# Scheduling a hybrid decoder layer with a second simulated machine: one flag on the tile context

## The chip, the cores and the metric

The kernel runs on one core of one Trainium2 chip. Its time is the device time of the program in microseconds (us), the median of three executions. One more execution was recorded by the hardware profiler. The engines are called PE (TensorE, matrix products), DVE (VectorE), ACT (ScalarE), POOL (GpSimd) and SP (SyncE, which here only issues transfers). PEld is the loading of a matrix product's stationary operand, which overlaps the PE.

## The reference

One decoder layer over 1024 positions of width 1024, all in 32-bit floats. Cut to what matters:

```python
z = rmsnorm(h, norm_mix_g) @ w_in                  # 1024 -> 3840 columns
o_a = hgrn2_mix(a_q, a_f, a_i, a_g, ...)           # 4 heads, gated linear recurrence
o_b = dilated_window_mix(b_q, b_k, b_v)            # 4 heads, three dilated causal windows
o_c = rwkv7_mix(c_in, ...)                         # 4 heads, RWKV-7 recurrence
h = h + concat(o_a, o_b, o_c) @ w_out
h = h + conv_glu_ffn(rmsnorm(h, norm_ffn_g), ffn_up, ffn_conv_w, ffn_conv_b, ffn_down)   # inner width 2816
h = h + sigmoid(rmsnorm(h, norm_ple_g) @ ple_gate) * (p @ ple_proj)
return rmsnorm(h, final_norm_g)
```

## The kernel before, in words

Every activation is held with features on the 128 partitions and positions along the row, in tiles of 128 x 512 (half of the positions) or 128 x 1024. A product of full precision is made of three products of a shorter float format: `split2` (L104 on ACT, L106 on POOL or DVE) cuts a weight tile into a high part `whi` and a low part `wlo`, and `mm3` (L127, L129, L131) adds high x high, high x low and low x high in one accumulator. Six buffers each hold `whi` and `wlo`, two hold a raw weight block `wraw` (512 KB, loaded on the SP queue at L95), and accumulators lie in the eight banks of the matmul memory (two of 128 x 1024 called `dp`, four of 128 x 512 called `mx`).

The stages follow each other:

1. `mix_norm` (L352 to L362) loads the input, makes its operands and the first projections while the norm is still being computed.
2. `rwkv` runs twice, once for each pair of heads: `rwkv_prep` (L478 to L542), `rwkv_inverse` (31 steps of two DVE instructions, L591 and L593, with trips through memory before and after), then `rwkv_main` in four groups of four chunks (L689 to L781). Projections of later blocks are written into the program between these (`project_rest`, 6, 4, 4 and 4 blocks) so that the PE has products to make while the DVE works through the inverse.
3. The HGRN2 heads run as two streams A (heads 0 and 2) and B (heads 1 and 3), the windowed attention as a stream C and the last projections as a stream F. `interleave` steps through these four generators in a fixed list, so their instructions alternate in the program. Inside a head, seven levels follow each other: ACT makes keys (L847), the PE makes scores (L857), the DVE puts them in place under a mask (L859) and scales queries (L862), DVE or POOL scales keys (L860). Then come the state chain (L901, L910), the output (L920, L922), its norm (L927 to L934) and its transposition (L940, L941). Stream C makes scores (L1001), a masked minimum (L1008), an exponential (L1010), transpositions (L1024, L1025) and values (L1037).
4. `phase_out` multiplies by `w_out` and starts the second norm.
5. `phase_up` computes the feed-forward's up-projection in 22 units of seven block products (L1148, Strassen-like), each unit with sums of weight blocks on the DVE (L1254 to L1262), additions out of the accumulators (L1292, L1301, L1303, L1311, L1313), the convolution (L1322 on ACT, L1323 and L1324 on DVE) and the gated product (L1331). The result goes to memory.
6. `phase_down` makes seven products of 11 steps (L1439) with the split of the reloaded operand (L1435, L1436).
7. `phase_ple` makes the gate (L1513 to L1516), the last norm, and writes the output (L1499, L1500).

No order of instructions is written out by hand for an engine. The program is traced in the order of the Python code, and the tile framework orders it when the `with tile.TileContext(nc)` block closes. It plays the program on a simulated machine with a clock. On each engine and on each transfer queue it takes, among the instructions whose operands the simulation says are there and whose buffers are free, the one that stands first in the program. The order in which the simulated machine takes them becomes the fixed order of that engine, and buffers are handed out in that order. Semaphore waits are added afterwards for every dependence, so the order on one engine is what is fixed and the time of each instruction is not. An engine's queue, and a transfer queue, runs strictly in that order: an instruction that waits holds back what stands behind it.

There are two simulated machines to choose from. The kernel before uses the framework's ordinary one. The other one, the timeline simulator, describes each instruction as a list of events on parts of an engine (its sequencer, a queue of issued instructions, the engine itself), on the transfer engines and on the memory interface that DVE and POOL share. It is chosen by one argument of the context.

## Time and profile before

| | |
|---|---|
| time, median of 3 runs | 1546.66 us |
| the three runs | 1538.52, 1546.66, 1549.97 us |
| span of the profiled execution, first to last instruction | 1541.8 us |
| instructions in it | 20120 |
| PE busy | 1478.3 us (96%), 7480 products |
| PEld busy | 1223.3 us (79%) |
| DVE busy | 1096.9 us (71%), 1578 instructions |
| ACT busy | 630.1 us (41%), 1079 instructions |
| POOL busy | 425.3 us (28%), 353 instructions |
| transfers | 167.83 MB, mean 109 GB/s |

The time of the profiled execution itself is not recorded beside its span; the span lies 4.9 us under the median of the three runs and between the lowest and the highest of them. In a row of the profile, "idle before" is the time that an engine stood still ahead of the instructions of that row, and the arrow names what ended the wait. A product's end is modelled, and products are pipelined, so the mean time of one (some 390 ns) is longer than the distance from one start to the next.

### The profile page before, as it was taken

The page shows a single profiled execution, that of the slowest core. Times are in us where ns is not written, and L with a number is a line of the kernel's source. Part 1 is how long each engine was busy: PE and PEld are TensorE (multiplying, and loading weights), DVE is VectorE, ACT ScalarE, POOL GpSimd, SP SyncE. Part 2 cuts the span into 40 slices and gives each one's busy share as a digit, 9 for nine tenths or more (in the row PEclk, how much of TensorE's full clock was granted, in tenths as well). Part 3 has the DMA queues.
Part 4 walks back from the last instruction along what each step waited for, and adds up shares of the span by engine and source line. Part 5 has one row for each costly group of instructions (what it writes and reads, how often), then busy time and mean ns, then how long its engine had stood idle before and what let it go on. Part 6 is the DMA issues. An engine that isn't in the chain of part 4 may idle for free.

```text
span 1541.8 us, 20120 instructions
## 1 busy us (share of the span) xinstructions
PE 1478.3 (96%) x7480; PEld 1223.3 (79%) x7480; DVE 1096.9 (71%) x1578; ACT 630.1 (41%) x1079; POOL 425.3 (28%) x353
## 2 busy tenths in 40 slices
PE   7999999999999989999999999999999999999996
PEld 5778988877977777777777888888888888888774
DVE  6567452656446567854788888888888799777684
ACT  6521331312323555523554444444444444455541
POOL 2233221323211113212214544444444000003230
PEclk9999999999999999999999999999999999999997
DMA  5124103124034132045342333333332883351352
GB/s 196 58 76 123 41 1 110 41 75 110 1 110 137 35 110 76 28 167 199 119 145 79 106 102 103 103 106 107 105 105 80 298 314 97 109 158 61 103 177 82
DMA packets 78706, 167.83 MB, mean 109 GB/s; under 512 B 19920, under 2 KB 20048, under 8 KB 78608
## 3 DMA queue, kind: packets, MB, share of 16 engines
q1 hardware_dynamic: 65120, 145.97, 29.0%
q10 hardware_dynamic: 12400, 16.52, 3.1%
q0 software_dynamic: 1088, 4.06, 0.8%
q8 instruction: 59, 0.97, 0.3%
q14 instruction: 39, 0.32, 0.1%
HBM read 120.12 MB, written 46.40 MB: 108 GB/s over the span
## 4 chain that ended last, share of the span: by engine, by line
PE 80%; DVE 8%; issue 5%; ACT 3%; DMA 2%; POOL 2%; POOLq 0%; SPq 0%; DVEq 0%; ACTq 0%
PE bg L1148 15%; PE bv L1148 11%; PE dp L131 7%; PE bv L1439 7%; PE bg L1439 7%; PE dp L129 7%; PE dp L127 7%; PE hsc L857 2%; PE swq L1001 1%; PE pgm L751 1%; PE swo L1037 1%; PE swt L1024 1%; PE zp L127 1%; PE zp L129 1%; PE zp L131 1%
## 5 line engine op out<-in xcount | busy, mean ns | idle before, releaser
L127 PE MATMUL dp<-xh,whi 128*128 128x512 f32 x544 | 185.1, 399 | 10.6 <-ACT xh L352 8.9
L131 PE MATMUL dp<-xh,wlo 128*128 128x512 f32 x544 | 184.7, 397 | 1.8 <-DVE wlo L106 1.5
L129 PE MATMUL dp<-xl,whi 128*128 128x512 f32 x544 | 185.9, 399 | 0.3 <-DVE xl L353 0.2
L106 POOL TENSOR_TENSOR wlo<-raw,whi 128x512 fp32r<-128x512 f32 x84 | 135.4, 1631 | 75.7 <-ACT whi L104 75.7
L104 ACT CAST whi<-wraw 128x512 fp32r<-128x512 f32 x120 | 73.3, 619 | 200.9 <-PE dp L129 136.1
L106 POOL TENSOR_TENSOR wlo<-wraw,whi 128x512 fp32r<-128x512 f32 x60 | 82.2, 1369 | 255.7 <-ACT whi L104 250.8
L1148 PE MATMUL bg<-t,whi 128*128 128x512 f32 x352 | 133.2, 389 | 0.0
L127 PEld LDWEIGHTS dp<-xh,whi 128*128 128x128 f32 x544 | 102.4, 190 | 33.1 <-ACT xh L352 8.9
L131 PEld LDWEIGHTS dp<-xh,wlo 128*128 128x128 f32 x544 | 103.4, 191 | 24.1 <-DVE wlo L106 2.0
L129 PEld LDWEIGHTS dp<-xl,whi 128*128 128x128 f32 x544 | 102.8, 190 | 24.3 <-DVE xl L353 2.5
L106 POOL TENSOR_TENSOR wlo<-s,whi 128x512 fp32r<-128x512 f32 x44 | 64.7, 1470 | 172.7 <-ACT whi L104 158.3
L1439 PE MATMUL bg<-t,whi 128*128 128x512 f32 x308 | 95.1, 390 | 0.0
L1439 PE MATMUL bv<-t,whi 128*128 128x512 f32 x308 | 94.9, 389 | 0.0
L104 ACT CAST whi<-raw 128x512 fp32r<-128x512 f32 x88 | 52.6, 619 | 96.8 <-issue 51.2
L104 ACT CAST whi<-s 128x512 fp32r<-128x512 f32 x66 | 38.9, 620 | 121.0 <-PE bg L1148 113.5
L167 POOL TENSOR_TENSOR rst<-rst,mhalf 128x4 f32<-128x4 f32 x8 | 9.3, 1158 | 251.6 <-DVE rst L161 251.5
L1148 PEld LDWEIGHTS bg<-t,whi 128*128 128x128 f32 x352 | 66.1, 188 | 13.8
L106 DVE TENSOR_TENSOR wlo<-wraw,whi 128x512 fp32r<-128x512 f32 x60 | 46.1, 773 | 41.8 <-ACT whi L104 34.7
L1439 PEld LDWEIGHTS bv<-t,whi 128*128 128x128 f32 x308 | 57.8, 188 | 12.0
L1148 PE MATMUL bg<-t,wlo 128*128 128x512 f32 x176 | 67.2, 389 | 0.0
L1439 PEld LDWEIGHTS bg<-t,whi 128*128 128x128 f32 x308 | 57.8, 188 | 11.8
L1435 ACT CAST t<-t 128x512 fp32r<-128x512 f32 x77 | 47.6, 621 | 44.5 <-PE bv L1439 31.1
(404 smaller groups left out, 3720.7 us busy)
## 6 DMA issues: line engine op xcount, KB each, us to landing
raw<-in_ffn_up_dram SPq DMA_DIRECT2D x44, 512.0 KB, 3.7
wraw<-in_w_in_dram SPq DMA_DIRECT2D x30, 512.0 KB, 3.7
z<-zst SPq DMA_DIRECT2D x18, 512.0 KB, 3.1
gb<-ct SPq DMA_DIRECT2D x33, 256.0 KB, 2.3
t<-gb SPq DMA_DIRECT2D x33, 256.0 KB, 2.8
t<-gt SPq DMA_DIRECT2D x33, 256.0 KB, 2.7
zl<-z SPq DMA_DIRECT2D x16, 512.0 KB, 4.2
wraw<-in_ple_gate_dram SPq DMA_DIRECT2D x16, 512.0 KB, 3.6
```

Source lines behind the costliest of these rows:

```text
L104: nc.scalar.copy(hi, src)
L106: eng.tensor_tensor(lo, src, hi.bitcast(F32), ALU.subtract)
L127: nc.tensor.matmul(ps[hf], wh, xh[hf], start=first, stop=False)
L129: nc.tensor.matmul(ps[hf], wh, xl[hf], start=False, stop=False)
L131: nc.tensor.matmul(ps[hf], wl, xh[hf], start=False, stop=last)
L751: nc.tensor.matmul(pg[:, u, :], X[:, 2 * hh + u, 0:128], RB[:, 2 * hh + u, :], start=True, stop=True)
L857: nc.tensor.matmul(sc[:, c, :], ks[:, c * P:(c + 1) * P], view(qt, c * P, [2 * n, 64 // n], [HT + n, 2], [1, n]), start=True, stop=True)
L1001: nc.tensor.matmul(pq[h][:, b:b + w], d["q"][hs, qb * P:nk], d["k"][hs, b:b + w], start=True, stop=True)
L1024: nc.tensor.transpose(pt[:, kb * P:(kb + 1) * P], lg[:, b + kb * P:b + (kb + 1) * P], self.ident)
L1148: nc.tensor.matmul(ps, w[part == 2][:, s], X[k][part == 1], start=start and k == part == 0, stop=k == 3 and part == 2, skip_group_check=no ...
L1435: nc.scalar.copy(xh, x)
L1439: nc.tensor.matmul(ps[m], wt[part == 2][:, m * P:(m + 1) * P], (xh, xl)[part == 1], start=k == part == 0, stop=k == NK - 1 and part == 2)
```

## The change

The context is built with one more argument. The traced program, its operations, tiles, pools and transfers stay as they are; the order of instructions on every engine and queue, and which of a pool's buffers a tile gets, come from the timeline simulator.

```diff
--- before.py
+++ after.py
@@ -1585,7 +1585,7 @@
         arrays[f"in_{name}_dram"] = v
         args[name] = nc.dram_tensor(f"in_{name}_dram", v.shape, mybir.dt.from_np(v.dtype), kind="ExternalInput").ap()
     out = nc.dram_tensor("out_0_dram", (ND, P, T), F32, kind="ExternalOutput").ap()
-    with tile.TileContext(nc) as tc:
+    with tile.TileContext(nc, schedule_with_timeline_sim=True) as tc:
         Trunk(tc, args, out).build()
     r = _run(nc, [arrays], core_ids=[0])
     y = r.results[0]["out_0_dram"]
```

## The prediction

> **What bounds the kernel now.** I read the page's busy times first, then the same by stage, then the chain that ended last, then the waits inside the one stage where the PE is not full.
>
> ```profile
> span 1541.8 us, 20120 instructions
> PE 1478.3 (96%) x7480; PEld 1223.3 (79%) x7480; DVE 1096.9 (71%) x1578; ACT 630.1 (41%) x1079; POOL 425.3 (28%) x353
> ...
> PE 80%; DVE 8%; issue 5%; ACT 3%; DMA 2%; POOL 2%; POOLq 0%; SPq 0%; DVEq 0%; ACTq 0%
> ```
>
> The PE is busy nearly always, and the chain runs through it for four fifths of the span. A product's recorded time overlaps the next one, so "busy" can hide short gaps. The rows by stage (busy us and number of instructions of PE, PEld, DVE, ACT, POOL, then the granted clock) show where.
>
> ```profile
> 0.00:30.00 30.00, 20.01 (x78) 14.60 (x79) 21.81 (x41) 22.41 (x40) 7.34 (x13) 1.00 0.69 241
> 60.00:100.00 40.00, 36.46 (x183) 29.16 (x183) 26.66 (x24) 13.87 (x21) 16.91 (x12) 0.91 0.11 39
> 100.00:150.00 50.00, 50.00 (x222) 41.36 (x222) 35.13 (x80) 9.92 (x17) 9.46 (x13) 1.00 0.41 111
> 270.00:330.00 60.00, 56.46 (x280) 45.81 (x279) 32.25 (x29) 18.75 (x27) 19.60 (x14) 0.94 0.19 57
> 480.00:580.00 100.00, 95.40 (x644) 76.54 (x643) 64.83 (x126) 49.57 (x100) 17.66 (x17) 0.97 0.22 77
> 580.00:680.00 100.00, 92.82 (x706) 75.09 (x705) 75.36 (x141) 49.17 (x97) 26.52 (x20) 0.97 0.17 53
> 811.00:1213.00 402.00, 401.59 (x1764) 332.22 (x1765) 351.79 (x362) 169.12 (x236) 190.25 (x122) 1.00 0.32 106
> 1213.00:1400.00 187.00, 187.00 (x827) 154.89 (x826) 156.69 (x251) 91.14 (x149) 0.00 (x0) 1.00 0.57 185
> 1500.00:1542.00 42.00, 26.42 (x116) 21.58 (x114) 20.73 (x30) 8.10 (x14) 3.95 (x3) 0.81 0.27 98
> ```
>
> From 811 to 1400 us (up and down projection) one product starts every 402 / 1764 = 228 ns and 187 / 827 = 226 ns, and the PE has no idle time. From 100 to 150 us it is 50 / 222 = 225 ns. That is the pace of a full array here. In such a stretch PEld is busy 332.22 / 402 = 0.826 of the time, so I use 0.826 as the mark of a full PE and convert the other rows with it. The whole span needs 1223.3 / 0.826 = 1481 us of PE; 61 us are not used. The start (30 - 14.60 / 0.826 = 12.3) and the end (42 - 21.58 / 0.826 = 15.9) hold 28 of them, 480 to 680 us holds 200 - 151.63 / 0.826 = 16.4, and 60 to 100 and 270 to 330 hold 4.7 and 4.5. The remaining 7 us are spread. **An order of instructions can win at most these 61 us, and some 33 us without touching start and end. It can lose much more**, since every gap that it opens where the PE is full counts whole.
>
> The stage from 480 to 680 us is where the order matters most: three chains (streams A, B, C) go round PE, DVE, ACT and POOL, and F's projections run out in it. Groups of that stage (first of its first half, then of its second):
>
> ```profile
> L857 PE MATMUL hsc<-qt,ks 128*128 128x128 f32 x112 | 16.0, 288 | 0.2 <-DVE qt L862 0.2
> ...
> L857 PE MATMUL hsc<-qt,ks 128*128 128x128 f32 x112 | 16.7, 297 | 1.5 <-DVE qt L862 1.5
> ...
> L862 DVE TENSOR_TENSOR qt<-qt,hT 128x512 f32<-128x512 f32 x12 | 10.4, 866 | 0.0
> L859 DVE COPY_PREDICATED hS<-cmask,hsc 128x512 f32<-128x512 uint8 x14 | 10.3, 737 | 4.6 <-PE hsc L857 4.4
> L1008 DVE CUSTOM_DVE_ANT_0 lg<-swq,swmask 128x384 f32<-128x384 f32 (+5 forms) x12 | 10.2, 885 | 3.1 <-PE swt L1024 3.1
> L847 ACT COPY ks<-hk 128x512 f32<-128x512 f32 x13 | 8.2, 639 | 8.6 <-PE hsc L857 4.0 <-PE swq L1001 2.6 <-POOL hk L860 1.7
> ...
> DVE hS L859 <- PE hsc L857: 18.3, 11, 6.3
> ```
>
> Heads and levels: 224 products of L857 are 8 for each of 28 levels, 14 levels one after the other in each of streams A and B. No single wait is long; the DVE, 65 to 75% busy, and the PE pass work to each other in pieces of 0.7 to 0.9 us.
>
> **The change, part by part.** Nothing is added or removed: the same 20120 instructions, the same bytes. What moves is the place of an instruction in its queue, on PE, DVE, ACT, POOL and the SP queue, wherever the two simulated machines disagree on what is ready first. A place can cost in one way only: an instruction that waits stands in front of one that could run. The trace of before has no row for an order that it did not run, so each part is bounded from both sides.
>
> *Up and down projection, 590 us of the span.* No gain is possible (PE full). I cost a loss at nothing, because the DVE has idle time to absorb a changed place: 402 - 351.79 = 50 us, over 402 / (84 x 0.227) = 21 units (seven block products of 12, at the pace above) 2.4 us each. What happens without that cover is a rival below.
>
> *SP queue.* Its waits are long already, and loads stand behind stores in it:
>
> ```profile
> SPq L95 <- DVE wlo L106: 332.3, 52, 37.1
> SPq L1340 <- DVE ct L1331: 61.3, 11, 15.2
> ...
> raw<-in_ffn_up_dram SPq DMA_DIRECT2D x44, 512.0 KB, 3.7
> ```
>
> A weight load of the up stage waits at most 15.2 us behind a store (L1340) and lands 3.7 us later, together 18.9 us. Four `raw` buffers are two units, 2 x 19 us, so one wait of this kind more per unit stays hidden. I take 0; if a load came in a full unit late, that is 19 us once, kept for the range.
>
> *RWKV stages, 60 to 480 us.* Here chains run beside projections that only need a free buffer. A projection block is 48 products x 0.227 = 10.9 us. Taking one earlier moves its work from a full stretch to one with 4.7 or 4.5 us of room: a gain of up to 4.5 each time, or a loss of 10.9 - 4.5 = 6.4 each time if the chain stands behind the block. For two pairs of heads that is -9 to +13. Between these I take 0, since PE work is not lost while projections are left.
>
> *HGRN2 and window stage, 480 to 680 us.* Per stream there are 14 levels and 16 further steps (transposition, state chain, output, norm, transposition, about 8 for each of two heads): 30 links in a row. If each link waits for one more piece of another stream, the piece is a DVE instruction such as L862 (866 ns) or L859 (737 ns), in the mean 0.80 us: 30 x 0.80 = 24 us. The upper end is two pieces of L1008, one after the other as stream C issues them for its two heads: 30 x 2 x 0.885 = 53 us. The lower end is the room found above, -16 us. I take **+24 us**. The reason for the sign: this stage's room is only 16.4 us of 200, so the order that ran is within 8% of the best possible here, while a different one is bounded below by nothing nearer than 53. The reason for the size: L862 and L859 are the rows that most often stand beside a link.
>
> The clock adds to this in principle. The granted clock is 0.97 in both halves of this stage and 0.81 in the last 42 us. The Trainium skill says (TensorE: Matmul & The Clock Gate, "What's actually happening") that an idle window of about 3.4 us halves the clock. The low clocks beside idle time agree with it in kind. By that rule, gaps collected into long ones would cost a second time: another 0.03 x 200 = 6 us, an estimate, and the sum would be 30 instead of 24. With gaps of 0.8 us it would not apply, so I leave it out.
>
> *Start and end.* The input's arrival and the output's last chain bound these. Price 0, from -10 to +10, a third of the 28 us of room either way.
>
> Sum: 0 + 0 + 0 + 24 + 0 = +24 us on the profiled span, 1565.8 us. The median of the runs is 4.9 us above that span (1546.66), so the time is **1570 us**, +1.5%. The forecast's own bounds are the mark of 1% (1562) and the upper end of the one term (1541.8 + 53 + 4.9 = 1600).
>
> **The rivals.**
>
> *No difference that counts* (within 1%, 1531 to 1562). A change of 1% is about what a measurement of this kernel can tell from none, as its three runs already span 0.7%. The two machines may agree almost everywhere, or the changed places fall where another stream fills the PE. For it: PE full in four fifths of the span, whatever stands in its queue. Against it: 16 us is enough to pass the mark, and 30 links need only half a microsecond each. Time: 1547 us. That the flag leaves the order as it is belongs here too.
>
> *Faster.* The timeline's picture of transfers, queues and the shared memory interface is closer to the chip, so an instruction that in truth waits no longer stands in front of one that is ready. The place is the same stage, plus 60 to 100 and 270 to 330. Half of the 33 us of inner room, and a third of the 28 us at the ends, is 16.5 + 9.3 = 26 us: 1521 us. For it: DVE waits 18.3 us for L857 in this stage and 3.1 us at L1008 for L1024, both waits behind which other DVE work stood. Against it: the room is small, and it must be won in several stages at once.
>
> *Much slower: the DVE becomes the bound of the up stage.* Forms of the same shape there:
>
> ```profile
> L1262 DVE TENSOR_TENSOR s<-s,raw 128x512 f32<-128x512 f32 x20 | 35.5, 1777 | 0.9 <-POOL wlo L106 0.9
> L1254 DVE TENSOR_TENSOR s<-raw,raw 128x512 f32<-128x512 f32 x20 | 33.3, 1664 | 0.7
> L1323 DVE SCALAR_TENSOR_TENSOR ct<-bv,ncw,ct 128x1023 f32<-128x1023 f32 x21 | 26.9, 1282 | 24.7 <-ACT ct L1322 24.7
> ...
> L1292 DVE TENSOR_TENSOR bg<-bg,v 128x512 f32<-128x512 f32 x21 | 14.7, 699 | 14.9 <-PE bg L1148 14.3
> ...
> L1257 DVE TENSOR_TENSOR raw<-raw 128x512 f32<-128x512 f32 x20 | 13.6, 682 | 0.0
> ```
>
> L1254 and L1262 take 1.66 and 1.78 us where L1257 takes 0.68, with the same shape. If the new order puts such a pair (3.4 us) or four pieces of convolution (4 x 1.28 = 5.1 us) ahead of the addition L1292 that hands an accumulator on, it exceeds the 2.4 us of idle time per unit by 1.0 to 2.7 us, in 22 units 22 to 59 us. It decides from 2.4 us of added wait per unit on. With the median that is 1569 to 1606 us, and about 1600 as one number with half of the 24 us of the mixed stage beside the middle of these; if the down stage (DVE 156.69 of 187 us) suffers in proportion, 1640 us. Against it: L1292 waits 14.3 us for the PE, so the DVE comes early there.
>
> The Trainium skill says (GPSIMD Engine Reference, "Specifications") that POOL shares its memory interface with the DVE and contends with DVE instructions that read two inputs from SBUF. The slow pair L1254 and L1262 agrees with it. By that rule an order that leaves more such DVE instructions beside POOL's splits slows the DVE without any wait that the profile names.
>
> **How the numbers follow.** The forecast (1562 to 1600) has 0.42, no difference 0.25, faster 0.19, much slower 0.14. The first is likeliest because the changed places are many, the room to win is small and the room to lose is not. Faster by over 1% is then 0.19, within 1% 0.25, slower 0.42 + 0.14 = 0.56. As both signs hold chances, the range reaches to both: from 1516 us (the faster case with some of the spread of the runs) to 1645 us (the DVE case with the down stage); some 0.05 lie below and 0.08 above. The forecast's own range is 1562 to 1600.
>
> **What would show it.** Right: from 811 to 1400 us still one product every 226 to 228 ns and no PE idle time; the HGRN2 and window stage some 24 us longer than 200, with PEld under 0.75 busy in it and DVE waits for L857 above 18.3 us. The DVE rival would show as PE waits at L1148 for L1292, L1303 or `wlo`, and fewer than 1764 products in 402 us. The faster case would show PEld above 0.79 in the mixed stage. The forecast would be wrong in its place if the RWKV stages lengthen instead: a projection block of 10.9 us in `rwkv_prep` and idle PE beside the inverse (L591, L593). It would be wrong in its size if one queue, SP above all, holds a whole stage back.

## The result, and the profile after

The changed kernel takes 1593.79 us (median of four runs, 1592.07 to 1599.48). The kernel before took 1546.15 beside it. The ratio on record is 1.0333, with a 95% interval of 1.0308 to 1.0357: **3.3% slower**, 51 us of the 1542 that the kernel before took in most later comparisons. The two medians alone give 1.0308, 48 us. The forecast was 1570 us, slower by 1.5%. In the experiments below, "better" and "worse" are differences to this 1.0333, one hundredth being 15.4 us; the intervals make such a difference uncertain by some 5 us, and against the 1.0308 of the medians each "better" would be 4 us smaller. Two kernels (t_hold, t_down_dve) had their profiled execution at a granted clock of 0.65 throughout, 2178 us long; those traces are left out and their ratios are from the other executions.

The page of the changed kernel's profile, its first lines and the chain by engine:

```profile
span 1597.7 us, 20154 instructions
...
PE 1489.9 (93%) x7480; PEld 1227.4 (77%) x7480; DVE 1085.2 (68%) x1578; ACT 637.9 (40%) x1079; POOL 421.2 (26%) x353
...
PE 83%; DVE 7%; issue 3%; ACT 3%; DMA 2%; POOL 1%; POOLq 0%; ACTq 0%; SPq 0%; DVEq 0%
```

The work is the same (7480 PE instructions, PEld 1227 against 1223 us, the same counts on DVE, ACT and POOL; the 34 instructions more in all are semaphore instructions), the chain still runs through the PE, and the span is 56 us longer. So PE time went unused. The next two fences are busy times by stretch, cut at the same instructions in both kernels: start, first preparation, first inverse, first main part with the projections behind it, second preparation, second inverse, second main part, HGRN2 and window stage, output projection, up, down, PLE stage, end. The columns are the stretch and its length, then busy us and instructions of PE, PEld, DVE, ACT, POOL, then the granted clock, DMA share and GB/s. Before:

```profile
0.00:58.50 58.50, 46.76 (x202) 36.57 (x202) 34.13 (x54) 36.19 (x57) 16.32 (x22) 1.00 0.49 167
58.50:97.50 39.00, 35.46 (x190) 29.25 (x189) 25.29 (x22) 13.50 (x20) 16.36 (x11) 0.91 0.09 28
97.50:150.60 53.10, 53.10 (x232) 43.27 (x231) 36.50 (x81) 10.89 (x19) 10.61 (x15) 1.00 0.41 114
150.60:278.80 128.20, 127.64 (x768) 111.37 (x766) 54.00 (x88) 37.02 (x86) 27.71 (x38) 1.00 0.17 54
278.80:319.70 40.90, 37.36 (x199) 30.80 (x199) 26.43 (x22) 14.25 (x22) 18.31 (x13) 0.92 0.08 26
319.70:372.40 52.70, 51.50 (x231) 41.90 (x230) 36.02 (x82) 9.95 (x18) 8.03 (x12) 1.00 0.41 115
372.40:479.30 106.90, 102.35 (x638) 90.01 (x637) 54.72 (x98) 34.13 (x85) 26.85 (x39) 0.97 0.24 79
479.30:682.00 202.70, 190.92 (x1366) 154.09 (x1365) 142.08 (x268) 99.36 (x198) 44.71 (x36) 0.97 0.20 68
682.00:786.40 104.40, 101.17 (x453) 82.41 (x452) 66.98 (x101) 44.70 (x74) 20.50 (x16) 1.00 0.52 182
786.40:1213.10 426.70, 423.94 (x1862) 350.03 (x1862) 370.54 (x389) 183.22 (x260) 196.48 (x126) 1.00 0.33 107
1213.10:1424.30 211.20, 210.75 (x936) 174.47 (x935) 175.68 (x276) 103.47 (x171) 10.43 (x7) 1.00 0.52 167
1424.30:1525.50 101.20, 94.39 (x410) 76.63 (x409) 68.01 (x91) 42.80 (x74) 27.99 (x20) 0.97 0.37 122
1525.50:1541.80 16.30, 2.98 (x12) 2.50 (x12) 6.46 (x11) 0.63 (x1) 1.01 (x1) 0.52 0.34 129
```

After:

```profile
0.00:63.20 63.20, 46.86 (x195) 37.03 (x196) 35.45 (x54) 36.45 (x57) 17.54 (x21) 0.97 0.45 155
63.20:108.60 45.40, 45.40 (x242) 36.57 (x241) 29.55 (x26) 15.72 (x24) 15.84 (x13) 1.00 0.15 47
108.60:157.80 49.20, 49.20 (x215) 40.05 (x215) 33.79 (x78) 8.80 (x15) 8.48 (x9) 1.00 0.41 121
157.80:298.40 140.60, 135.25 (x790) 117.93 (x789) 53.81 (x88) 39.27 (x89) 30.71 (x43) 0.98 0.14 47
298.40:347.90 49.50, 36.61 (x177) 27.53 (x176) 23.87 (x24) 12.88 (x20) 14.87 (x12) 0.79 0.10 33
347.90:394.40 46.50, 46.50 (x203) 37.78 (x203) 33.49 (x79) 9.14 (x16) 8.97 (x9) 1.00 0.39 110
394.40:507.30 112.90, 102.21 (x644) 87.98 (x642) 51.71 (x98) 35.92 (x89) 27.23 (x43) 0.95 0.22 79
507.30:719.10 211.80, 194.63 (x1390) 157.70 (x1388) 144.26 (x270) 100.31 (x194) 47.91 (x36) 0.98 0.17 58
719.10:827.40 108.30, 100.99 (x420) 81.14 (x421) 63.46 (x91) 42.59 (x70) 20.21 (x16) 0.93 0.52 185
827.40:1252.20 424.80, 418.07 (x1837) 345.52 (x1836) 360.12 (x394) 185.94 (x260) 189.47 (x126) 0.99 0.32 105
1252.20:1487.30 235.10, 220.82 (x960) 181.97 (x960) 178.45 (x280) 106.51 (x172) 7.04 (x6) 0.96 0.48 156
1487.30:1581.90 94.60, 91.14 (x410) 74.51 (x409) 70.75 (x94) 43.71 (x76) 31.97 (x22) 1.00 0.39 128
1581.90:1597.70 15.80, 2.17 (x12) 1.69 (x12) 6.50 (x11) 0.63 (x1) 1.01 (x1) 0.58 0.35 133
```

A stretch may be longer because it holds more work. So I take the prediction's mark: the growth of PEld divided by 0.826 is the work that came in, and the rest of the growth in length is PE time lost there. Where products are short, as in the two main parts, this split is rough: before, PEld is busy 111.37 of 128.20 us in the first, 0.869, more than the mark.

| stage | growth | work moved in | lost |
|---|---|---|---|
| start | +4.7 | +0.6 | +4.1 |
| first preparation | +6.4 | +8.9 | -2.5 |
| first inverse | -3.9 | -3.9 | 0.0 |
| first main part | +12.4 | +7.9 | +4.5 |
| **second preparation** | +8.6 | -4.0 | **+12.6** |
| second inverse | -6.2 | -5.0 | -1.2 |
| second main part | +6.0 | -2.5 | +8.5 |
| HGRN2 and window | +9.1 | +4.4 | +4.7 |
| output projection | +3.9 | -1.5 | +5.4 |
| up | -1.9 | -5.5 | +3.6 |
| **down** | +23.9 | +9.1 | **+14.8** |
| PLE stage and end | -7.1 | -3.6 | -3.5 |
| sum | +55.9 | +5.0 | +51.0 |

Start and RWKV stages hold 26 of the 51 us, the down stage 15, the stage that the prediction named 4.7. How much of each belongs to the order of that stage, only experiments can say.

Two waits show what the large losses look like. Waits of the changed kernel in the second preparation, then a group of projection products in it (count, busy us, mean ns):

```profile
PE dp L127 <- DVE r L429: 12.9, 1, 12.9
```

```profile
L129 PE MATMUL dp<-xl,whi 128*128 128x512 f32 x30 | 11.3, 462 | 0.0
```

The kernel before has 36 products in that group at 407 ns:

```profile
L129 PE MATMUL dp<-xl,whi 128*128 128x512 f32 x36 | 11.7, 407 | 0.0
```

Each projection block has 16 of these, so 36 are 2.25 blocks and 30 are 1.9. The new order has fewer products there, and the PE stands 12.9 us in one piece, waiting for the DVE to read an accumulator `dp`. From the chain that ended last in the changed kernel (start, us, what):

```profile
317.31 6.46 DVE ig L504 x2
...
325.75 1.21 DVE r L429
```

The product that waits belongs to the next projection block (L386 reads its result later). Both accumulators `dp` hold blocks of the second pair itself, for its `r` and `v`, and the DVE reads `r` only after the reciprocals L504 of its chain. So a block was at hand and had no accumulator. In the kernel before, the PE was still making the block for `v` during L504.

In the down stage the PE stands at the seam between the first and the second of the seven products. Its waits in the changed kernel between 1200 and 1320 us follow; the kernel before and t_down below have none there.

```profile
PE bg L1439 <- ACT whi L104: 10.5, 1, 10.5
PE bg L1439 <- DVE wlo L106: 3.7, 1, 3.7
```

What it waits for stands in the chain that ended last (the two pieces of the DVE), and in the order of the SP queue:

```profile
1289.15 6.66 DVE h L1448 x11
...
1301.14 3.09 DVE sr L1395 x5
```

```profile
1262.26 10.39 SPq L1456 DMA_DIRECT2D h<-hd  x16
...
1284.29 4.84 SPq L1394 DMA_DIRECT2D wa<-in_ffn_down_dram  x8
```

The DVE first adds the results of the first product into `h` (L1448), then sums the weight blocks of the second (L1395), and then come the splits that the PE waits for. The first of the loads `wa` for these sums is issued 32.1 us after the first down product, behind sixteen reloads of `h`. It lands at 1289.5 us, 2 us after the first product has ended. The sums begin only at 1296.9. In the kernel before, `wa` comes 18.5 us after the first down product, and the DVE makes its first sum before its first addition:

```profile
1231.63 0.33 SPq L1394 DMA_DIRECT2D wa<-in_ffn_down_dram  x1
```

```profile
1237.94 0.69 DVE L1395 TENSOR_TENSOR t<-t,wa 128x512 f32<-128x512 f32 x1
...
1243.71 3.67 DVE L1448 TENSOR_TENSOR h<-h,bg 128x512 f32<-128x512 f32 x6
```

The longest wait of a store in the SP queue is no part of this. It is the tenth of the eleven stores at L1340 in both kernels, 15.2 us long before and 15.1 after, and after the change it ends at 1233 us, while the PE is full. In two stretches of the changed kernel's down stage:

```profile
1252.00:1300.00 48.00, 37.45 (x162) 30.68 (x161) 37.01 (x56) 17.24 (x26) 0.00 (x0) 0.91 1.01 362
1310.00:1487.00 177.00, 177.00 (x785) 146.59 (x784) 131.35 (x209) 85.94 (x140) 6.85 (x5) 1.00 0.35 103
```

From 1252 to 1300 the PE makes 162 products in 48 us. Later it makes 785 in 177 us, one every 225 ns.

### The profile page after: what moved, and what is told of

Read it like the earlier page. It is cut to its first block, busy times and chain, and to the rows that moved or that the text cites. A ratio compares the mean times of both kernels' runs of the same rounds, so it can differ in the third digit from the quotient of the medians.

```text
span 1597.7 us, 20154 instructions
## 1 busy us (share of the span) xinstructions
PE 1489.9 (93%) x7480; PEld 1227.4 (77%) x7480; DVE 1085.2 (68%) x1578; ACT 637.9 (40%) x1079; POOL 421.2 (26%) x353
## 4 chain that ended last, share of the span: by engine, by line
PE 83%; DVE 7%; issue 3%; ACT 3%; DMA 2%; POOL 1%; POOLq 0%; ACTq 0%; SPq 0%; DVEq 0%
PE bg L1148 15%; PE bv L1148 11%; PE dp L127 8%; PE dp L131 8%; PE dp L129 8%; PE bg L1439 7%; PE bv L1439 7%; PE swq L1001 1%; PE hsc L857 1%; PE swt L1024 1%; PE swo L1037 1%; PE pgm L751 1%; PE zp L127 1%; PE zp L129 1%; PE zp L131 1%
## 5 line engine op out<-in xcount | busy, mean ns | idle before, releaser
L127 PE MATMUL dp<-xh,whi 128*128 128x512 f32 x544 | 189.5, 408 | 38.2 <-DVE r L429 12.9
L131 PE MATMUL dp<-xh,wlo 128*128 128x512 f32 x544 | 189.7, 407 | 2.5 <-POOL wlo L106 1.7
L129 PE MATMUL dp<-xl,whi 128*128 128x512 f32 x544 | 190.6, 407 | 0.5 <-DVE xl L353 0.5
L127 PEld LDWEIGHTS dp<-xh,whi 128*128 128x128 f32 x544 | 106.1, 197 | 62.6 <-DVE r L429 13.1
L106 POOL TENSOR_TENSOR wlo<-raw,whi 128x512 fp32r<-128x512 f32 x84 | 125.2, 1505 | 84.3 <-ACT whi L104 84.3
L1148 PE MATMUL bg<-t,whi 128*128 128x512 f32 x352 | 121.5, 391 | 0.0
L1439 PE MATMUL bg<-t,whi 128*128 128x512 f32 x308 | 96.5, 396 | 10.5 <-ACT whi L104 10.5
L106 DVE TENSOR_TENSOR wlo<-wraw,whi 128x512 fp32r<-128x512 f32 x60 | 51.8, 866 | 42.2 <-ACT whi L104 32.4
L1148 PEld LDWEIGHTS bg<-t,whi 128*128 128x128 f32 x352 | 66.6, 189 | 14.0
L1148 PE MATMUL bg<-t,wlo 128*128 128x512 f32 x176 | 68.1, 390 | 0.0
```

The costliest lines, as they stand in the source:

```text
L106: eng.tensor_tensor(lo, src, hi.bitcast(F32), ALU.subtract)
L127: nc.tensor.matmul(ps[hf], wh, xh[hf], start=first, stop=False)
L129: nc.tensor.matmul(ps[hf], wh, xl[hf], start=False, stop=False)
L131: nc.tensor.matmul(ps[hf], wl, xh[hf], start=False, stop=last)
L1148: nc.tensor.matmul(ps, w[part == 2][:, s], X[k][part == 1], start=start and k == part == 0, stop=k == 3 and part == 2, skip_group_check=no ...
L1439: nc.tensor.matmul(ps[m], wt[part == 2][:, m * P:(m + 1) * P], (xh, xl)[part == 1], start=k == part == 0, stop=k == NK - 1 and part == 2)
```

## The experiments

Most kernels build the program twice, with the ordinary and with the timeline's simulator. They read the order of every queue from the first build and fix parts of the second to it. The fixing adds a place in the queue and no wait (cut short):

```diff
+def pin(tc, nc, order, marks):
+    for engine, first, last in PINS:
+        queue = [n for n in order[engine] if n in traced and marks[first] <= traced[n][0] < marks[last]]
+        for a, b in zip(queue, queue[1:]):
+            tc.add_manual_dep(traced[b][1], a, NoSync)
...
+    nc = build(True, order_of(build(False)))
```

The line with `build` is for the kernels with t_ (timeline, parts put back); those with o_ swap the two builds (ordinary, parts taken from the timeline). Marks stand where `build`, `phase_mix` and `rwkv` begin a stage or a part of one. `ALL` stands for the five queues. "Lag" is the time of an instruction in a trace minus its time in the trace of before.

**The RWKV stages put back, and the same piece taken alone.**

```diff
+PINS = [(e, None, 'mixed') for e in ALL]   # t_rwkv, and o_rwkv with the builds swapped
```

> Timeline order, but every queue's instructions that are traced before the HGRN2 and window stage stand in the order of the kernel before. Theory R (the RWKV stages run out of projections, because the new order puts 5.9 of the 6.5 blocks that are left into the first pair of heads, and the rest of the loss comes in the HGRN2 stage, w_out and the down stage): the lag of 22 to 28 us at the end of the RWKV stages goes, 1594 - 25 = 1569 us. Theory M (the prediction's: the loss is in the chains of the HGRN2 and window stage, the RWKV stages are within -9 and +13): at most 13 us better, 1581 to 1594.

Measured 1.0152 (1.0127 to 1.0177): 28 us better. The lag at the first score of the HGRN2 stage (L836) is 6.3 us instead of 28.0, and 5.9 of that is nothing: o_ple below, which has before's order up to the PLE stage, shows the same 5.9 in its own trace. Theory R's number, and past theory M's 13. It is more than the 26 - 6 = 20 us that the table then leaves for these stages, because the output projection recovers too: from L836 to the first up product the lag grows by 5 us (6.3 to 11.5) where it grew by 13 (28.0 to 41.0).

> Ordinary order, but every queue's instructions that are traced before the HGRN2 and window stage in the timeline's order. Theory R (that order costs by itself, whatever stands behind it): 20 to 28 us slower than before, 1562 to 1570. Rival (it costs only together with what the timeline moves up from later stages): within 8 us of before, 1542 to 1550.

Measured 1.0178 (1.0155 to 1.0202), 27 us slower than the kernel before. From both sides the order of these stages costs 27 to 28 us, by itself.

**Which queue in the RWKV stages.**

```diff
+PINS = [('PE', None, 'mixed')]    # t_rwkv_pe
+PINS = [('DVE', None, 'mixed')]   # t_rwkv_dve
```

> Timeline order, but PE's instructions that are traced before the HGRN2 and window stage stand in the order of the kernel before (the other queues stay with the timeline, as far as PE's order lets them). Theory R (which projection block stands where on PE decides): as good as all five queues pinned there, some 27 us better, 1566 us, and the second pair of heads starts with projections left. Rival (the chains' own queues, DVE above all, decide, and the blocks only follow): no more than 8 us better, 1586 to 1594.

Measured 1.0271 (1.0241 to 1.0300): 10 us better, a third of what was expected. PE in the old order then waits for the other queues, which come in the new one: its waits for `bb` from ACT before the inverse (L568) grow from 7.1 us to 11.5.

> Timeline order, but DVE's instructions that are traced before the HGRN2 and window stage stand in the order of the kernel before. Theory R: DVE issues the splits of the weights for the projections too, so its order holds the blocks back with it, but PE is free to take them early: 0 to 15 us better, 1579 to 1594. Rival (DVE's order is the cause): 23 us better or more, 1571 or less.

Measured 1.0286 (1.0259 to 1.0312): 7 us better, inside theory R's range, and far from the rival. Neither queue alone carries the loss. "Which block stands where on PE decides" was too simple: an order is an agreement between queues.

**Holding blocks back.** This one leaves all queues to the timeline and ties only the PE instructions between the two pairs of heads (four projection blocks, and the second half's norm of the first pair) behind the first pair's main part:

```diff
+    last = pe("main0", "late0")[-1].name
+    for i in pe("late0", "prep1"):
+        tc.add_manual_dep(i, last, NoSync)
```

> Timeline order on every queue, with one thing held back: PE may take the four projection blocks that stand between the two pairs of heads only after the last PE instruction of the first pair. Theory R (the second pair's preparation starves because these blocks have gone): in the trace PE's unused time in the preparation of the second pair falls from 20 to 8 us, the length of the first pair's main part from 128 to 80-85 us, and the time is 12 to 18 us better, 1576 to 1582. Rival (the chain's own order on DVE and ACT makes the second preparation long): blocks are there, but the stretch is no shorter in unused PE time, 1590 to 1598.

Measured 1.0255 (1.0237 to 1.0273): 12 us better, the edge of the expectation. The same kernel was run again for a trace:

> The same kernel as t_hold, for a trace: four projection blocks held back on PE until the first pair is done. Time as measured, 1580 to 1583. Theory R: PE's unused time in the preparation of the second pair 8 us instead of 20, and 12 of the gain lie there. Rival: that stretch still leaves 15 us or more, and the gain is in the first pair's main part, whose products no longer stand between the links of the chain.

Measured 1.0249 (1.0229 to 1.0270). (The expectations count PE's unused time by products, which gives 20 us where the table's measure gives 49.5 - 27.53 / 0.826 = 16.2.) Its stretches of the first main part and of the second preparation, and the group of products in the latter:

```profile
158.20:293.50 135.30, 129.49 (x761) 112.77 (x762) 53.66 (x87) 37.93 (x87) 29.66 (x42) 0.99 0.13 44
293.50:336.90 43.40, 43.40 (x233) 34.90 (x232) 30.09 (x25) 14.55 (x22) 14.77 (x11) 1.00 0.15 49
```

```profile
L130 PE MATMUL dp<-xl,whi 128*128 128x512 f32 x48 | 15.2, 395 | 0.0
```

The second preparation now has three blocks instead of 1.9, no idle PE, a clock of 1.00 instead of 0.79, and 43.4 - 34.90 / 0.826 = 1.1 us unused. The first pair's main part alone, from its first L689 to its last L775, takes 69 us where it took 123 (70 before), more of a change than the expected 80 to 85: the new order had made blocks inside it. So this much is shown: **12 to 13 of the 28 us came from projections that the new order had spent too early.** That the PE then stood with a block at hand and no free accumulator is what the trace adds. The rest of the 28 us is not tied to one cause.

**The prediction's stage.**

```diff
+PINS = [(e, 'mixed', 'up') for e in ALL]    # t_mixed_out
+PINS = [(e, 'mixed', 'out') for e in ALL]   # t_mixed
+PINS = [(e, 'out', 'up') for e in ALL]      # t_out
```

> Timeline order, but every queue's instructions of the HGRN2 and window stage and of the output projection in the order of the kernel before. Theory R: the trace shows 9 us more length in the one and 5 in the other, so 14 better, 1580 us. Theory M: 24 us better, 1570.

Measured 1.0258 (1.0242 to 1.0273): 12 us better, nearer to R's 14 than to M's 24, and it doesn't say which of the two stages.

> Timeline order, but every queue's instructions of the HGRN2 and window stage alone in the order of the kernel before. Theory R (that stage lost 4 to 5 us of PE; the other 7 us of its greater length are 0.65 of a projection block that was moved into it): 0 to 5 us better, 1589 to 1594. Theory M (the prediction's): 24 us better, 1570.

Measured 1.0356 (1.0339 to 1.0374): no better, rather 3 us worse. The old order of the HGRN2 and window stage is worth nothing here; put back together with the output projection it may be worth 12 - 6 = 6 us (t_mixed_out against t_out, next), within what such a difference can tell, and far from 24. **The term on which the forecast stood is refuted.**

> Timeline order, but every queue's instructions of the output projection alone in the order of the kernel before. Theory O (the order there costs by itself: DVE's sums for the up stage stand in front of its work and wait for raw): 8 to 10 us better, 1584 to 1586. Rival (the loss there is handed on from the stages before, since pinning the RWKV stages alone took 8 us out of it too): 0 to 4 us better, 1590 to 1594.

Measured 1.0296 (1.0276 to 1.0316): 6 us better, between the two. In the traces the lag at the first down product falls from 39.2 to 27.3 us. The cause that I had named did not go: DVE's sum still waits 2.3 us for `raw` in that kernel, 2.2 in the changed one. So the order there costs some 6 us, and what it costs them for is open.

**The down stage.**

```diff
+PINS = [(e, 'up', None) for e in ALL]           # t_down
+PINS = [('SP', 'down', None)]                   # t_down_sp
+PINS = [('PE', 'up', None)]                     # t_down_pe
+PINS = [('PE', 'up', 'ple'), ('SP', 'up', 'ple')]   # t_down_pesp
+PINS = [('DVE', 'up', 'ple')]                   # t_down_dve
```

> Timeline order, but every queue's instructions from the up projection to the end in the order of the kernel before. Theory R: the lag grows from +41 us at the first up product to +63 at the last down product and falls to +56 at the end, so 15 better, 1579 us. Theory M: nothing, 1590 to 1594, as these stages keep PE full in any order.

Measured 1.0293 (1.0274 to 1.0313): 6 us better. The lag does not grow at all in the down stage (40.6 us at its first and its last product, against 39.2 and 63.0), so with all five queues in the old order the stall is gone. The old order of the PLE stage came with it and takes 7 us of that back: from the last down product to the last L1516 the lag falls by 6.6 us in the changed kernel (63.0 to 56.4) and grows by 0.5 here. By the profiled spans the kernel is 14.5 us better (1583.2 against 1597.7). The profiled execution of the changed kernel was the slowest of its four, so the ratio, 6 us, is the safer number. With t_rwkv and t_mixed_out, the three pieces that make up the program give 28 + 12 + 6 = 46 of the 51 us, each uncertain by some 5.

> Timeline order, but the SP queue alone from the down projection on in the order of the kernel before. Theory S (the down stage stalls because its first weights wa stand behind 8 to 10 loads of t and behind the ws loads in the SP queue): the stall of 18 us goes, 1576 us. Rival (the stall is in the order of the splits on DVE, ACT and POOL, whi and wlo for the same product, and SP only follows): within 4 us of the changed kernel, 1590 to 1594.

Measured 1.0307 (1.0278 to 1.0337): 4 us better. The stage's lag grows by 17 instead of 24 us. Theory S named at most a part of it.

> Timeline order, but PE alone from the up projection on in the order of the kernel before. Theory C (the new PE order takes the first down product p1 ahead of the last up products; that makes the last unit's convolution late by 6.5 us and uses up the work that covers the t and wa loads): the stall of the down stage loses at least 10 of its 20 us, but the end stage loses its 6 to 10 us of gain as well, 1582 to 1590 us; in the trace the lag grows by less than 10 us from the first to the last down product. Rival (SP's order alone, wa behind t): the stall stays, lag +20 or more in that stage, 1594 to 1600.

Measured 1.0372 (1.0343 to 1.0401): 6 us worse. In the trace the lag grows by 12, so the theory's sign is right for the stage (and its "less than 10" is missed). But the first down product is 2.8 us later, and the PLE stage gives nothing (54.2 to 55.1). In the spans that adds up to 1 us better, in the times to the wrong side.

> Timeline order, but PE and SP together from the up projection to the end of the down projection in the order of the kernel before; the PLE stage stays with the timeline. PE alone took 12 of the 24 us from the growth of the lag in the down stage, SP alone 7. Theory S+C (the wa loads behind the t loads and the products taken too early are two halves of one stall): together at least 18 us, the lag grows by at most 6, 1593.8 - 18 = 1576 us. Rival (the order of the splits on DVE and ACT holds the rest): the lag still grows by 10 or more, 1580 to 1590.

Measured 1.0300 (1.0282 to 1.0317): 5 us better, and the lag still grows by 9.8. The rival, that DVE and ACT hold the rest, is nearer, and the DVE's additions L1448 still hold the largest share of the chain at the seam in this trace.

> Timeline order, but the loads of wa in the down projection are issued on POOL's queue instead of SP's, so they stand behind no t load. Theory S (that wait is what SP's order costs): as much as pinning SP from there, the lag in the down stage grows by 17 us or less instead of 24, 7 us better or more, 1582 to 1588. Rival (t itself comes late, from the late last unit of the up stage): growth of the lag 22 or more, 1590 to 1595.

```diff
-            nc.sync.dma_start(W1[k], block(k, 2, 1))
+            nc.gpsimd.dma_start(W1[k], block(k, 2, 1))
```

Measured 1.0351 (1.0336 to 1.0367): no better. The lag grows by 20.5, between the two. `wa` was issued 22 us earlier, counted from the first down product (9.7 us behind it instead of 32.1), and not earlier, because POOL had to wait for the last up product (L1148). The PE still waits, 12.3 us now:

```profile
PE bg L1439 <- ACT whi L104: 12.3, 1, 12.3
```

```profile
1259.57 17.21 SPq L1456 DMA_DIRECT2D h<-hd  x16
```

The transfers are not free of each other: the sixteen reloads of `h` on SP's queue take 17.2 us instead of 10.4, and the `t` loads behind them come late (ACT waits up to 7.7 us for one). `wa` itself lands after 8.4 us instead of 5.4 (medians from 1240 to 1300 us). And the DVE again makes its sixteen additions L1448 first, to 1296 us, though `wa` was there. Early loads alone are of no use to an order of the DVE that comes back to them late.

> Timeline order, but DVE alone from the up projection to the end of the down projection in the order of the kernel before. Theory D (DVE puts a split of the first down product after every piece of the last unit's convolution, at PE's pace; so its stores wait, by 15.1 us for the longest, and the t and wa loads behind them on SP): the longest wait of SP for the convolution falls under 5 us, the lag grows by at most 10 us instead of 24, 14 us better, 1580 us. Rival (PE's and SP's places hold the stall whatever DVE does): growth 17 or more, 1587 to 1595.

Measured 1.0423 (1.0402 to 1.0443): 14 us worse. Theory D as a repair by one queue falls, and the wait of 15.1 us that it starts from is in the kernel before too. Without a trace that can be used, where DVE's old order then waited is open. What stands is the whole: all five queues together remove the stall, and neither PE, SP nor DVE alone does; how the loss divides between the late loads and the DVE's order is open.

**A version that beats both.** The timeline's PLE stage lost less PE time than before's, and so did its first preparation. These kernels start from the ordinary order:

```diff
+PINS = [(e, 'ple', None) for e in ALL]          # o_ple
+PINS = [(e, None, 'main0') for e in ALL] + [(e, 'ple', None) for e in ALL]   # o_prep2
+PINS = [(e, None, 'main0') for e in ALL] + [(e, 'up', 'down') for e in ALL] + [(e, 'ple', None) for e in ALL]   # o_prep_up_ple
```

> Ordinary order, but every queue's instructions of the PLE stage at the end in the timeline's order. By the trace of the changed kernel the lag falls by 7 to 10 us in that stage, so 1536 us, 0.4 to 0.6% faster than the kernel before. Rival (the lag falls there only because the stall before it had left work of this stage undone or done early): within 2 us of before.

Measured 0.9974 (0.9956 to 0.9992): 4 us faster than the kernel before, as far as the interval reaches.

> Ordinary order, but the timeline's on every queue up to the first pair's main part (start, preparation and inverse of the first pair, with the six projection blocks behind them) and in the PLE stage. In the traces the first preparation leaves 1.7 us of PE unused with the timeline and 6.4 to 7.1 without, the start 23 against 17 to 21: -2 us, and -4 from the PLE stage, so 1536 us, 0.4% faster than before. If the blocks that are taken early are missed later (as in the second pair), 1 to 5 us slower than before.

Measured 0.9967 (0.9955 to 0.9979). Faster than before, and not to be told from o_ple.

> As o_prep2, and the timeline's order of the up stage too (its own instructions only). By the traces in which that stage leaves 2.3 us of PE unused instead of 5.2: 1535 us, 0.5% faster than before. If the order of the last unit goes with the order of the down stage, its loads come late again: 1542 or more.

Measured 0.9937 (0.9921 to 0.9952), 1533.99 us: **0.6% faster than the kernel before** and the best version seen. The up and the PLE stage by stretch:

```profile
788.10:1212.10 424.00, 422.36 (x1862) 349.20 (x1861) 361.50 (x391) 186.98 (x260) 184.89 (x126) 1.00 0.33 109
1423.30:1517.80 94.50, 91.14 (x410) 74.57 (x409) 67.56 (x91) 42.51 (x74) 28.78 (x20) 1.00 0.39 130
```

The up stage leaves 424.0 - 349.20 / 0.826 = 1.2 us of PE unused where before's stretch left 426.7 - 350.03 / 0.826 = 2.9; the PLE stage 94.5 - 74.57 / 0.826 = 4.2 where before left 101.2 - 76.63 / 0.826 = 8.4.

## Why the prediction was wrong

The sign was right, for a reason that held: little room to win (the best mixture found 10 of the 61 us) and much to lose. The size and the place were wrong. That 1594 us lies inside the forecast's own bounds, 1562 to 1600, is luck: their upper end was built from the HGRN2 and window stage, whose order a run puts at nothing.

*HGRN2 and window stage, +24 us: the failed step.* It counted one more piece of 0.80 us on each of 30 links. Such a piece never appeared: DVE's wait for L857 went from 18.3 to 14.3 us, where over 18.3 was to show it. After the change, in that stage:

```profile
DVE hS L859 <- PE hsc L857: 14.3, 11, 4.5
```

The trace gives 4.7 us lost, and the run that put the stage back gives none. PEld did fall under 0.75 busy (157.70 / 211.80 = 0.745), but it was only 154.09 / 202.70 = 0.760 before, so that sign told little. My reading, which no run shows by itself, is that three streams and F's blocks on one PE absorb a changed place as long as another one is ready.

*RWKV stages, 0 within -9 and +13, and start, 0 within -10 and +10: mis-sized.* Together they cost 27 to 28 us, beyond both upper ends. The step priced one block out of place at 6.4 us. It missed that the blocks are a fixed stock, and the timeline spends it early: taking a block costs nothing where it is taken, and later a stretch that had been covered stands bare, or has a block and both accumulators taken. That is 12.6 us in one preparation, of which holding four blocks back recovered all in that stretch. The prediction's own sign for this, "a projection block of 10.9 us in `rwkv_prep`", was the wrong way round: the second preparation had less of them, not more.

*SP queue, 0, with 19 us once for a late load.* For the wait that it named, 0 was right: that wait is the same in both kernels (15.2 us before, 15.1 after), inside a full stretch. Late loads had a part in a loss at a place that the step did not look at: the seam between the first two down products, where no unit is in hand. The down stage lost 14.8 us by the table, near the 19 kept for the range, but by another way, so the nearness is luck. "If one queue, SP above all, holds a whole stage back" names too little: SP's own order was only a part of it.

*Up and down, 0: mis-sized for down.* From 870 to 1250 us the PE did not stand (380 us, 1679 products, 226 ns), as said, and the 2.4 us of added wait per unit that the DVE rival needed never came. But "the DVE has idle time to absorb a changed place" was worked out for units of the up stage and taken for the down stage as well. At the seam there the DVE has sixteen additions and eleven sums in a row to do, some 0.6 us each, before the PE is full again, and with the loads late and the additions in front nothing covers them. There the DVE ends last, not the PE.

*Start and end, 0.* 4.1 us lost at the start in this trace; the trace of o_ple has 3.4 us of lag at the same point with before's order, so most of it is nothing. PLE stage and end won 3.5, which the version above kept.

*No difference* and *faster* didn't come as a whole, though both were there by stage: the mixed stage moved nothing, and the timeline's first preparation, up and PLE stages are better than before's.

## What to carry to other kernels

Where a full engine is fed from a stock of independent work, count the stock by stretch, and the accumulators that it needs, not the places: an order that spends it early looks good until the stretch that has none. Seams between stages, where the next one's first operands are the last one's results, are priced by what stands in front of those operands in every queue, here sixteen reloads on SP and sixteen additions on the DVE, and not by how full the stages on both sides are. And an order need not be taken whole: put back stage by stage, it showed which stages were better in it, and a mixture beat both.

## What the runs showed of the hardware

The granted clock cost more than the prediction allowed, where idle time came in one piece. Stretches of the changed kernel around the wait of 12.9 us, and around the stall in the down stage:

```profile
306.00:319.00 13.00, 8.10 (x54) 5.61 (x52) 5.36 (x5) 7.63 (x8) 1.41 (x1) 0.89 0.06 11
319.00:328.00 9.00, 1.00 (x2) 0.83 (x3) 9.00 (x8) 0.00 (x0) 2.17 (x1) 0.50 0.11 45
...
1284.00:1296.00 12.00, 3.77 (x17) 2.80 (x15) 9.34 (x16) 1.24 (x2) 0.00 (x0) 0.79 1.05 394
...
1304.00:1312.00 8.00, 6.51 (x16) 5.21 (x17) 8.00 (x15) 1.86 (x3) 0.00 (x0) 0.57 0.00 2
1312.00:1330.00 18.00, 18.00 (x81) 14.85 (x80) 18.00 (x31) 8.11 (x13) 0.00 (x0) 1.00 0.31 89
```

The PE stands from 314.1 to 327.0 us, and from 319 on the clock is 0.50. After the stall, 16 products take 6.51 us, 407 ns each, at 0.57, and then 81 take 18 us, 222 ns each, at 1.00. PEld as a whole grew by 4.1 us, which is 5.0 us of PE at 0.826: by this estimate, the second cost of gaps that come in one piece. The Trainium skill (TensorE: Matmul & The Clock Gate, "What's actually happening") has the clock halve after an idle window of about 3.4 us; the 0.50 agrees with the halving, the length of the window is not measured here, and this kernel's gaps of 10 to 13 us are what the prediction had ruled out with "gaps of 0.8 us".

In the stall the transfers run at 394 GB/s with a DMA share of 1.05, and a load of 256 KB (`wa`) lands 5.4 us after its issue, where one of 512 KB for the up stage (`raw`) takes 3.8: the late loads also took longer. The Trainium skill (Perfetto Trace Analysis, "Roofline") puts the bound of one core's 16 DMA engines near 435 GB/s; the 394 over these 12 us agree with such a bound.

The slow pair of additions in the up stage goes with POOL: in the kernel before, all 22 of L1257 and 21 of 22 of L1256 run while POOL is idle and take 0.68 to 0.69 us, and L1262 takes 1.75 to 1.78 us, with POOL busy for most of each. The rival that this would slow the DVE in the new order did not come: DVE busy fell from 1096.9 to 1085.2 us.
